# Other PSUM banks for one feed-forward block, another form of the RMS norm in two mixers, operand sums inside the first group of the kernel, and 24 matmuls ahead of it

## The chip, the cores and the metric

One core of a Trainium2 chip runs the whole program. The metric is device time in microseconds of one execution, from inputs in HBM to outputs in HBM. TensorE (PE) runs at one of two clocks, 1.2 or 2.4 GHz; the profile gives the granted one as a share of the upper.

## What is computed

A trunk of two macaron layers over x of shape (1, 512, 1024) in float32, each layer a half-weighted SwiGLU feed-forward block, a mixer, and another half-weighted feed-forward block:

```
def rmsnorm(x, g):
    y = x * lax.rsqrt(jnp.mean(x * x, axis=-1, keepdims=True) + EPS)
    return y * g

def swiglu(x, w_in, w_out):            # w_in (1024, 2*2816), w_out (2816, 1024)
    gate, up = jnp.split(x @ w_in, 2, axis=-1)
    return (jax.nn.silu(gate) * up) @ w_out

for i in range(2):                      # mixer 0: attention over keys that an indexer picks; mixer 1: gMLP
    h = h + 0.5 * swiglu(rmsnorm(h, norm_g[i, 0]), ffn_w_in[i, 0], ffn_w_out[i, 0])
    h = h + mixer_i(rmsnorm(h, norm_g[i, 1]))
    h = h + 0.5 * swiglu(rmsnorm(h, norm_g[i, 2]), ffn_w_in[i, 1], ffn_w_out[i, 1])
return rmsnorm(h, final_g)
```

## The kernel before

**Layout.** Activations lie transposed: eight tiles `H[j]`, each 128 features by 512 tokens. Every product is made of three float32r matmuls (`mul3`, L366 to L368): operand x and weight w are split into a high part (`xh`, `whi`, a rounding copy on ScalarE, ACT) and the rest (`xl`, `wlo`, a subtraction on VectorE, DVE), and PE adds wh·xh, wh·xl and wl·xh into one PSUM bank. `prepare(j)` (L321) makes `xh`, `xl` and the squares of one tile; the opening of the kernel does it by `weigh` and `square` (L302, L308). `H` itself is not scaled by the norm before a product: the token's 1/rms is multiplied onto the product afterwards (`R["b"]`).

**Weights.** `WeightStream` brings weights in units of eight 128x128 pieces in the exact order of use. SP's queue loads a unit into one of four `raw` tiles, ACT makes `whi` (L183), DVE `wlo` (L186). For plain units the converted parts have three places: a unit is converted only when PE has left the unit three before it. The program is written out by hand; each engine executes its instructions strictly in the order in which the code issues them.

**A feed-forward block** (`ffn`, L409), four of them, for layer and norm numbers 0, 2, 3 and 5: a first `group` takes four products at once, eight k-steps of twelve matmuls; then four `single` products; then nine `two_pairs`, each seven products (f0 to f6) of 24 matmuls of 256 columns, a Strassen-like form that uses sums of halves of the operands (`TH`, `TL`, made by `sums`, L441, four sets, one for each pair of tiles); and three times an output product into `H` (`add`, L640: DVE reads the bank at L642, adds at L643, then `finish` prepares that tile for the next stage). Blocks two to four make three sets at k-steps 5 to 7 of their first group and the fourth behind the first `single`; the first block makes one set behind each of its four singles.

**PSUM** is two sets of four banks, tags `acc` and `aux`, each handed out in turn. A block begins with four `acc` banks for its first group and takes `aux` for the singles. Its last product ends on `acc` for features 4 to 7, and the group of what follows begins on `acc` too, both between the second and third feed-forward block and between the third block and the gMLP mixer.

**Norms.** In the feed-forward blocks the sum of squares over features is made by columns (`scale_columns`, L391: four float32 matmuls of one column, which show as eight instructions), the reciprocal root on a 128x4 tile (L292 to L297), and the spread over all partitions by `scale_rows` (L399). The mixers use `token_scale` (L341): two float32r matmuls with a matrix of ones that sum all 512 columns into every partition, the root on a 128x512 tile, and later `as_columns` (L354), four transposes, for the factor by token.

**The opening.** SP's queue loads the first weight unit in two halves, the tiles `H[j]` and three more units; the norm gains `g_sb` come by the queue of GpSimd (POOL).

Of the kernel before, what the change touches and what calls it, by code (L numbers as in the profile page):

```python
# [50 lines left out]
LAST = 2 * CHUNKS[-1]  # L51
N_LOADS = sum(4 if k == "S" else 1 for k in PLAN)
# [188 lines left out]
def tile_trunk(ctx: ExitStack, tc, specs_out, xT, wst, gT, gl, rel, onehot, bu, bv, lng, lnb, wspT, bsp, out):  # L241
# [29 lines left out]
    pad(small, 32)  # L271
    g_sb = const.tile([P, 7, KD], F32, name="g_sb")
    nc.gpsimd.dma_start(g_sb, gT)
# [11 lines left out]
    nc.scalar.activation(ones_r, ones, AF.Copy)  # L285

# [54 lines left out]
    def token_scale(tag="aux"):  # L341

        ah = small.tile([P, S], F32R, tag="s0_512", bufs=1, name=uname("ah"))
        al = small.tile([P, S], F32R, tag="s1_512", bufs=1, name=uname("al"))
        nc.scalar.activation(ah, acc[0], AF.Copy)
        nc.vector.tensor_tensor(al, acc[0], ah.bitcast(F32), op=ALU.subtract)
        ps = bank(tag)
        mm(ps, ones_r, ah, start=True, stop=False)
        mm(ps, ones_r, al, start=False, stop=True)
        v = small.tile([P, S], F32, tag="ms", bufs=1, name=uname("ms"))  # L350
        nc.vector.tensor_scalar(v, ps, 1.0 / D, EPS, op0=ALU.mult, op1=ALU.add)
        return rsqrt(v, [P, S])

    def as_columns(rb):  # L354

        ps = bank("aux")
        for t in range(NT):
            nc.tensor.transpose(ps[:, t * P:(t + 1) * P], rb[:, t * P:(t + 1) * P], ident)
        c = small.tile([P, NT], F32, tag="rcol", bufs=1, name=uname("rcol"))
        nc.vector.tensor_copy(c, ps.rearrange("p (t q) -> p t q", q=P)[:, :, 0])  # L360
        return c

# [28 lines left out]
    def scale_columns(ps):  # L391

        for t in range(NT):
            mm(ps[:, t:t + 1], acc[0][:, t * P:(t + 1) * P], ones[:, :1], start=True, stop=True)
        v = small.tile([P, NT], F32, tag="vcol", bufs=1, name=uname("vcol"))
        nc.vector.tensor_scalar(v, ps[:, :NT], 1.0 / D, EPS, op0=ALU.mult, op1=ALU.add)
        return rsqrt(v, [P, NT])

    def scale_rows(rc, ps):  # L399
# [4 lines left out]
        rh = small.tile([P, S], F32, tag="ms", bufs=1, name=uname("rh"))  # L404
        nc.scalar.activation(rb, ps, AF.Copy)
        nc.scalar.activation(rh, ps, AF.Copy, scale=0.5)  # L406
        return rb, rh

    def ffn(layer, which, norm, finish, begin=None, hooks=None, aside=None, last=None):  # L409
# [8 lines left out]
        KP = KD // 2  # L418
        n1, n2 = slice(0, HALF), slice(HALF, S)
        with tc.tile_pool(name=uname("ffn"), bufs=1) as fp:  # L420
# [67 lines left out]
            def plain_pairs(banks, g, begun=0):  # L488
                for i in range(begun, 2):
                    nc.vector.tensor_tensor(g[:, i], banks[2 * i], R["b"], op=ALU.mult)  # L490
# [66 lines left out]
            def scale():  # L557
                R["ps"] = R.get("ps") or bank("aux")
                R["c"] = scale_columns(R["ps"])
# [16 lines left out]
            rest = [bank("aux") for _ in range(2)]  # L576
            if not hooks:
                plain_pairs(banks, g[0])
            else:
                R["ps"] = bank("aux")  # L580
            single(rest[0], 2, KD, spec_in)
# [7 lines left out]
            rest.append(bank("aux"))  # L589
# [647 lines left out]
```

## Time and profile before

| | us |
|---|---|
| median of 3 runs (2110.95 to 2118.17) | 2111.97 |
| the profiled execution, its own time | 2112.86 |
| its span, first to last instruction | 2110.8 |
| PE busy | 2076.8 (98%) |
| DVE busy | 1487.5 (70%) |
| ACT busy | 891.3 (42%) |
| mean granted clock | 0.997 |

The stretches of the span on PE: opening group and singles 0 to 57 us, the rest of the first feed-forward block to 364, attention mixer to 626, second block to 974, third to 1326, gMLP mixer to 1749, fourth block to the end. Matmuls are pipelined: the next one starts before the modelled end of the one before, so a group's pace is read from starts.

### The profile page before, as it was taken

What the parts mean: (1) busy time and instruction counts of PE and PEld (TensorE: products, weight loads), DVE (VectorE), ACT (ScalarE), POOL (GpSimd) and SP (SyncE); (2) the same over time, 40 slices, a digit from 0 to 9 for tenths busy, and PEclk for the clock granted to TensorE, in tenths of its full rate; (3) what the DMA queues carried; (4) which work ended last, traced back from release to release, by engine and by line L of the source; (5) the groups of instructions that cost most, each with busy time, mean ns of one, the idle gap of its engine ahead of it and who ended that gap; (6) DMA issues with size and microseconds to landing.
All of it is one profiled execution on the core that took longest, in us unless ns stands there. A gap on an engine that the chain in (4) does not pass through costs nothing.

```text
span 2110.8 us, 29664 instructions
## 1 busy us (share of the span) xinstructions
PE 2076.8 (98%) x12208; PEld 1839.1 (87%) x12208; DVE 1487.5 (70%) x2044; ACT 891.3 (42%) x1151; POOL 78.8 (4%) x58
## 2 busy tenths in 40 slices
PE   8999999999999999999999999999999999999998
PEld 6889898788888999897889999788888888989897
DVE  6868686697767677676868677645746466768686
ACT  5535344434445345344625344322323245435253
POOL 0000000143200000000000000000000000000000
PEclk9999999999999999999999999999999999999999
DMA  4233332222122222222323222422232222323221
GB/s 172 97 116 109 110 110 99 90 96 94 61 80 100 100 100 101 100 100 80 108 95 117 100 101 80 141 100 80 91 109 80 91 90 90 108 93 110 104 96 70
DMA packets 58887, 209.70 MB, mean 99 GB/s; under 512 B 6696, under 2 KB 6760, under 8 KB 58624
## 3 DMA queue, kind: packets, MB, share of 16 engines
q1 hardware_dynamic: 55584, 198.73, 26.9%
q0 software_dynamic: 1440, 5.41, 0.8%
q10 hardware_dynamic: 1728, 3.67, 0.5%
q8 instruction: 95, 1.56, 0.3%
q14 instruction: 40, 0.33, 0.1%
HBM read 205.67 MB, written 4.74 MB: 100 GB/s over the span
## 4 chain that ended last, share of the span: by engine, by line
PE 88%; DVE 7%; ACT 3%; issue 2%; DMA 0%; ACTq 0%; DVEq 0%; POOLq 0%
PE acc L366 15%; PE acc L367 15%; PE acc L368 15%; PE aux L366 10%; PE aux L367 10%; PE aux L368 10%; DVE wlo L186 1%; ACT whi L183 1%; PE aux L979 1%; PE aux L980 1%; PE aux L981 1%; PE aux L1031 1%; PE acc L979 1%; PE acc L980 1%; PE acc L981 1%
## 5 line engine op out<-in xcount | busy, mean ns | idle before, releaser
L186 DVE TENSOR_TENSOR wlo<-raw,whi 128x1024 fp32r<-128x1024 f32 (+1 forms) x382 | 464.2, 1219 | 309.7 <-ACT whi L183 308.2
L183 ACT ACTIVATE whi<-raw 128x1024 fp32r<-128x1024 f32 (+1 forms) x409 | 426.5, 1050 | 485.1 <-PE acc L367 203.7
L366 PE MATMUL acc<-xh,whi 128*128 128x256 f32 (+1 forms) x888 | 305.7, 344 | 8.9 <-ACT xh L305 5.9
L367 PE MATMUL acc<-xl,whi 128*128 128x256 f32 (+1 forms) x888 | 296.4, 334 | 0.1
L368 PE MATMUL acc<-xh,wlo 128*128 128x256 f32 (+1 forms) x888 | 296.3, 334 | 0.0
L366 PEld LDWEIGHTS acc<-xh,whi 128*128 128x128 f32 x888 | 169.5, 191 | 27.5 <-ACT xh L305 5.9
L366 PE MATMUL aux<-xh,whi 128*128 128x256 f32 (+1 forms) x592 | 190.7, 322 | 1.2 <-ACT rh L406 1.2
L368 PE MATMUL aux<-xh,wlo 128*128 128x256 f32 (+1 forms) x592 | 190.5, 322 | 1.3 <-DVE wlo L186 1.3
L367 PE MATMUL aux<-xl,whi 128*128 128x256 f32 (+1 forms) x592 | 190.2, 321 | 0.0
L366 PE MATMUL acc<-th,whi 128*128 128x256 f32 x640 | 181.8, 284 | 7.5 <-ACT u L519 6.0
L367 PEld LDWEIGHTS acc<-xl,whi 128*128 128x128 f32 x888 | 169.5, 191 | 18.2 <-issue 1.4
L368 PEld LDWEIGHTS acc<-xh,wlo 128*128 128x128 f32 x888 | 169.3, 191 | 16.7
L367 PE MATMUL acc<-tl,whi 128*128 128x256 f32 x640 | 181.2, 283 | 0.4 <-DVE tl L389 0.4
L368 PE MATMUL acc<-th,wlo 128*128 128x256 f32 x640 | 181.1, 283 | 0.0
L366 PE MATMUL aux<-th,whi 128*128 128x256 f32 x512 | 144.9, 283 | 0.0
L367 PE MATMUL aux<-tl,whi 128*128 128x256 f32 x512 | 144.9, 283 | 0.0
L368 PE MATMUL aux<-th,wlo 128*128 128x256 f32 x512 | 144.9, 283 | 0.0
L366 PEld LDWEIGHTS acc<-th,whi 128*128 128x128 f32 x640 | 122.8, 192 | 8.5 <-ACT u L519 6.8
L366 PE MATMUL acc<-yh,whi 128*128 128x512 f32 x328 | 127.7, 389 | 0.0
L367 PE MATMUL acc<-yl,whi 128*128 128x512 f32 x328 | 127.7, 389 | 0.0
L366 PE MATMUL aux<-yh,whi 128*128 128x512 f32 x328 | 127.6, 389 | 0.0
L367 PE MATMUL aux<-yl,whi 128*128 128x512 f32 x328 | 127.6, 389 | 0.0
(296 smaller groups left out, 4383.1 us busy)
## 6 DMA issues: line engine op xcount, KB each, us to landing
raw<-in_wst SPq DMA_DIRECT2D x372, 512.0 KB, 3.3
dist<-dist_rows ACTq DMA_DIRECT2D x8, 320.0 KB, 4.3
h<-in_xT SPq DMA_DIRECT2D x8, 256.0 KB, 6.8
tb<-dist POOLq DMA_DIRECT2D x8, 256.0 KB, 3.8
bias<-in_bv POOLq DMA_DIRECT2D x1, 1536.0 KB, 7.5
raw<-in_wst SPq DMA_DIRECT2D x2, 256.0 KB, 3.3
wT<-in_wspT POOLq DMA_DIRECT2D x1, 512.0 KB, 9.3
bs<-in_bsp POOLq DMA_DIRECT2D x1, 512.0 KB, 11.3
```

Of the source, the lines that this page charges most:

```text
L183: self.nc.scalar.activation(hi[:, s], src[:, s], AF.Copy)
L186: self.lo_engine.tensor_tensor(lo[:, s], src[:, s], hi[:, s].bitcast(F32), op=ALU.subtract)
L366: mm(ps, wh, xh, start=first, stop=False, **kw)
L367: mm(ps, wh, xl, start=False, stop=False, **kw)
L368: mm(ps, wl, xh, start=False, stop=last, **kw)
L979: mm(banks[t], xh, wh, start=k == 0, stop=False)
L980: mm(banks[t], xl, wh, start=False, stop=False)
L981: mm(banks[t], xh, wl, start=False, stop=k == KD - 1)
L1031: mm(ps[:, t * P:(t + 1) * P], V[t][:, d * P:(d + 1) * P], wT[:, g, :], start=True, stop=True)
```

## The change

- The third feed-forward block is called with `tags=("aux", "acc")`: wherever a block takes `acc` it now takes `aux` and the other way round.
- `token_scale` and `as_columns` are gone. Both mixers use columns: three hooks of their first group split the squares (`parts_of_squares`), sum them by columns and spread them by rows at k-steps 4, 5 and 6. In feed-forward blocks the split stands at k-step 3.
- `scale_columns` takes the split squares: eight float32r matmuls with two columns of ones in place of four float32 ones with one column.
- The first block makes all four sets of operand sums inside its first group, at k-steps 4 to 7; its norm is summed after the first single and spread after the second, and the special copy of its first single's bank is gone.
- 24 matmuls of 128x128 ones stand ahead of all others on PE; `g_sb` is loaded by ACT's queue instead of POOL's; a pad in the pool `small` is 64 bytes instead of 32.

```
+WARM = 24
-    pad(small, 32)
+    pad(small, 64)
-    nc.gpsimd.dma_start(g_sb, gT)
+    nc.scalar.dma_start(g_sb, gT)
...
+    warm = bank("aux")
+    for _ in range(WARM):
+        mm(warm[:, :P], ones_r, ones_r, start=True, stop=True)
...
-    def scale_columns(ps):
+    def parts_of_squares():
+        ah = small.tile([P, S], F32R, tag="s0_512", bufs=1, name=uname("ah"))
+        al = small.tile([P, S], F32R, tag="s1_512", bufs=1, name=uname("al"))
+        split(acc[0], ah, al)
+        return ah, al
+
+    def scale_columns(ps, parts):
         for t in range(NT):
-            mm(ps[:, t:t + 1], acc[0][:, t * P:(t + 1) * P], ones[:, :1], start=True, stop=True)
+            for part in parts:
+                mm(ps[:, 2 * t:2 * t + 2], part[:, t * P:(t + 1) * P], ones_r[:, :2], start=part is parts[0],
+                   stop=part is parts[1])
...
+    def norm_hooks(R, ps, k):
+        def parts():
+            R["sq"] = parts_of_squares()
+        def columns():
+            R["c"] = scale_columns(ps, R["sq"])
+        def rows():
+            R["b"], _ = scale_rows(R["c"], ps, False)
+        return {k: parts, k + 1: columns, k + 2: rows}
...
             def hook(k):
                 if hooks:
                     hooks[k]()
-                elif k in (5, 7):
-                    (scale if k == 5 else spread)()
-                if k > 4 and not hooks:
-                    sums(k - 5)
+                elif k == 5:
+                    scale()
+                elif k == 7:
+                    spread()
+                elif k == 3:
+                    R["sq"] = parts_of_squares()
+                if k > 3 + (not hooks):
+                    sums(k - 4 - (not hooks))
-            banks = [bank() for _ in range(4)]
+            banks = [bank(tags[0]) for _ in range(4)]
...
             single(rest[0], 2, KD, spec_in)
-            sums(0) if hooks else sums(3)
+            if hooks:
+                R["sq"] = parts_of_squares()
+                scale()
+            else:
+                sums(3)
             step()
             single(rest[1], NJ + 2, KD, spec_in)
             if hooks:
-                scale()
-                sums(1)
+                spread()
+                plain_pairs(banks, g[0])
...
-            if hooks:
-                spread()
-                nc.vector.tensor_tensor(g[1][:, 0], rest[0], R["b"], op=ALU.mult)
-                plain_pairs(banks, g[0])
-                sums(2)
...
-            group([kw] + pq, ["kw"] + [QI0 + P * i for i in range(4)], KD, spec_a, hooks={4: scale})
+            group([kw] + pq, ["kw"] + [QI0 + P * i for i in range(4)], KD, spec_a, hooks=norm_hooks(R, ps, 4))
...
-    ffn(1, 0, 3, into(4))
+    ffn(1, 0, 3, into(4), tags=("aux", "acc"))
```

The order of instructions moves at three places that matter below. In the rows, numbers behind names tell buffers apart, and lines of the changed kernel are its own (its L348 to L350 are L366 to L368 before, L310 is L306, L187 is L186).

PE at the end of the second feed-forward block and the start of the third, before: the last matmuls of the output product, then the first group on four `acc` banks.

```order
L367 MATMUL acc_9007<-yl_8788,whi_8909 128x512
L368 MATMUL acc_9007<-yh_8787,wlo_8910 128x512
L366 MATMUL acc_9052<-xh_80,whi_8948 128x512
L367 MATMUL acc_9052<-xl_88,whi_8948 128x512
L368 MATMUL acc_9052<-xh_80,wlo_8949 128x512
L366 MATMUL acc_9053<-xh_80,whi_8948 128x512
```

The same place of PE after the change.

```order
L349 MATMUL acc_9053<-yl_8834,whi_8955 128x512
L350 MATMUL acc_9053<-yh_8833,wlo_8956 128x512
L348 MATMUL aux_9098<-xh_80,whi_8994 128x512
L349 MATMUL aux_9098<-xl_88,whi_8994 128x512
L350 MATMUL aux_9098<-xh_80,wlo_8995 128x512
L348 MATMUL aux_9099<-xh_80,whi_8994 128x512
```

The order of work is the same; the group no longer begins on the set of banks that the output product ends on.

DVE in the opening group, before: the operand rests `xl` of tiles 6 and 7, the adding of squares, and weight units 5 and 6 of the stream.

```order
L306 SCALAR_TENSOR_TENSOR xl_94<-h_77,g_sb,xh_86 128x512
L317 TENSOR_TENSOR sqacc_171<-sqacc_171,sq_304 128x512
L186 TENSOR_TENSOR wlo_308<-raw_183,whi_307 128x1024
L306 SCALAR_TENSOR_TENSOR xl_95<-h_78,g_sb,xh_87 128x512
L317 TENSOR_TENSOR sqacc_171<-sqacc_171,sq_329 128x512
L317 TENSOR_TENSOR sqacc_171<-sqacc_171,sq_344 128x512
L186 TENSOR_TENSOR wlo_353<-raw_208,whi_352 128x1024
```

DVE at the same place after the change, from the last row of the first set of sums on.

```order
L371 TENSOR_TENSOR tl_168<-u_32_318,th_164 128x512
L310 SCALAR_TENSOR_TENSOR xl_94<-h_77,g_sb,xh_86 128x512
L321 TENSOR_TENSOR sqacc_196<-sqacc_196,sq_343 128x512
L455 TENSOR_TENSOR u_36_348<-m_34_346 128x256
L456 TENSOR_TENSOR u_36_348<-m_35_347,m_34_346 128x256
L457 TENSOR_TENSOR u_37_349<-m_35_347,u_36_348 128x256
L458 TENSOR_TENSOR u_37_349<-m_35_347,u_37_349 128x256
L371 TENSOR_TENSOR tl_169<-u_36_348,th_165 128x512
L371 TENSOR_TENSOR tl_169<-u_37_349,th_165 128x512
L187 TENSOR_TENSOR wlo_361<-raw_208,whi_360 128x1024
L310 SCALAR_TENSOR_TENSOR xl_95<-h_78,g_sb,xh_87 128x512
```

One set of sums, six instructions, now stands ahead of `xl` of tile 6, and a second one ahead of `xl` of tile 7. On ACT the high parts `xh` of the same tiles stand behind the same sets.

PE in the attention mixer's first group, before: the end of k-step 4, the two matmuls of `token_scale`, the start of k-step 5.

```order
L368 MATMUL aux_3497<-xh_84,wlo_3529 128x512
L348 MATMUL acc_3601<-ah_3597,ones_r 128x512
L349 MATMUL acc_3601<-al_3598,ones_r 128x512
L366 MATMUL acc_3493<-xh_85,whi_3528 128x512
L367 MATMUL acc_3493<-xl_93,whi_3528 128x512
```

PE there after the change: the end of k-step 5, the column sums, the start of k-step 6. Behind k-step 6 four instructions of `scale_rows` follow.

```order
L350 MATMUL aux_3531<-xh_85,wlo_3563 128x512
L384 MATMUL acc_3527<-ones_r,ah_3631 128x2
L384 MATMUL acc_3527<-ones_r,al_3632 128x2
L384 MATMUL acc_3527<-ones_r,ah_3631 128x2
L384 MATMUL acc_3527<-ones_r,al_3632 128x2
L384 MATMUL acc_3527<-ones_r,ah_3631 128x2
L384 MATMUL acc_3527<-ones_r,al_3632 128x2
L384 MATMUL acc_3527<-ones_r,ah_3631 128x2
L384 MATMUL acc_3527<-ones_r,al_3632 128x2
L348 MATMUL acc_3526<-xh_86,whi_3562 128x512
```

The sums stand one k-step, fifteen matmuls, behind the split of the squares instead of right behind it.

## Rows read from the trace of the kernel before

**Rows 1.** Part 1 of the page: busy time, share of the span, instructions.
```profile
PE 2076.8 (98%) x12208; PEld 1839.1 (87%) x12208; DVE 1487.5 (70%) x2044; ACT 891.3 (42%) x1151; POOL 78.8 (4%) x58
```

**Rows 2.** Timeline of PE, third block's start: start, duration, instruction [idle before, releaser].
```profile
975.16 0.39 PE L367 MATMUL acc<-xl,whi 128*128 128x512 f32 x1
975.39 0.39 PE L368 MATMUL acc<-xh,wlo 128*128 128x512 f32 x1
977.19 0.50 PE L366 MATMUL acc<-xh,whi 128*128 128x512 f32 x1 [1.42 <-DVE gate L642]
...
979.79 0.50 PE L366 MATMUL acc<-xh,whi 128*128 128x512 f32 x1 [1.63 <-DVE gate L642]
```

**Rows 3.** Timeline of PE, the start of the gMLP mixer.
```profile
1329.45 0.50 PE L979 MATMUL acc<-whi,xh 128*128 128x512 f32 x1 [1.42 <-DVE gate L642]
...
1332.04 0.50 PE L979 MATMUL acc<-whi,xh 128*128 128x512 f32 x1 [1.63 <-DVE gate L642]
```

**Rows 4.** Windows: stretch, length, busy us (instructions) by engine, granted clock, DMA.
```profile
383.68:387.10 3.42, 3.42 (x10) 2.65 (x9) 3.25 (x6) 0.00 (x0) 0.00 (x0) 0.50 0.35 135
...
977.50:981.00 3.50, 1.87 (x8) 1.23 (x7) 3.46 (x6) 1.75 (x3) 0.00 (x0) 1.00 0.45 150
...
1332.60:1336.00 3.40, 3.40 (x9) 2.63 (x8) 3.40 (x6) 2.19 (x3) 2.65 (x5) 0.50 0.45 112
```

**Rows 5.** Timeline of DVE at the third block's start, tile 7 and a weight unit.
```profile
981.64 0.74 DVE L333 SCALAR_TENSOR_TENSOR xl<-h,g_sb,xh 128x512 fp32r<-128x512 f32 x1
...
982.91 1.22 DVE L186 TENSOR_TENSOR wlo<-raw,whi 128x1024 fp32r<-128x1024 f32 x1
```

**Rows 6.** Timeline of PE, norms of the attention mixer and, last, the gMLP mixer.
```profile
380.53 0.39 PE L368 MATMUL aux<-xh,wlo 128*128 128x512 f32 x1
...
383.02 0.50 PE L349 MATMUL acc<-al,ones_r 128*128 128x512 f32 x1 [0.84 <-DVE al L346]
383.36 0.39 PE L366 MATMUL acc<-xh,whi 128*128 128x512 f32 x1
...
401.32 0.60 PE L358 MATMUL aux<-ident,nwy 128*128 128x128 f32 x4
...
1346.15 0.50 PE L349 MATMUL aux<-al,ones_r 128*128 128x512 f32 x1 [0.40 <-DVE al L346]
```

**Rows 7.** Timeline of PE, norm by columns in the third feed-forward block.
```profile
994.21 0.95 PE L394 MATMUL aux<-ones,sqacc 128*128 128x1 f32 x8
...
1000.56 1.05 PE L402 MATMUL aux<-ident,nwy 128*128 128x128 f32 x8
```

**Rows 8.** The opening: issue of the fourth weight unit, and `xl` of tile 3.
```profile
5.93 0.71 SPq L107 DMA_DIRECT2D raw<-in_wst  x1
...
16.75 0.75 DVE L306 SCALAR_TENSOR_TENSOR xl<-h,g_sb,xh 128x512 fp32r<-128x512 f32 x1
```

**Rows 9.** View by tile (raw), window of that one issue: time to landing.
```profile
DMA to landing us min/median/max: 8.5/8.5/8.5
```

**Rows 10.** Windows in the opening, columns as in rows 4.
```profile
6.00:9.00 3.00, 3.00 (x7) 2.02 (x8) 2.07 (x3) 1.76 (x3) 0.00 (x0) 1.00 0.98 330
```

**Rows 11.** Timeline of DVE and ACT: `xl` of tile 7, and one set of sums.
```profile
28.75 0.75 DVE L306 SCALAR_TENSOR_TENSOR xl<-h,g_sb,xh 128x512 fp32r<-128x512 f32 x1
...
54.03 1.32 ACT L446 ACTIVATE m<-h,g_sb 128x512 f32<-128x512 f32 x2
...
56.52 1.48 DVE L389 TENSOR_TENSOR tl<-u,th 128x512 fp32r<-128x512 f32 x2
```

**Rows 12.** Timeline of PE: f0 and f4 of the first pairs, first and second block.
```profile
57.22 0.28 PE L366 MATMUL acc<-xh,whi 128*128 128x256 f32 x1
...
73.99 0.39 PE L366 MATMUL acc<-th,whi 128*128 128x256 f32 x1 [2.72 <-ACT u L519]
...
671.73 0.28 PE L366 MATMUL acc<-xh,whi 128*128 128x256 f32 x1
...
684.49 0.39 PE L366 MATMUL acc<-th,whi 128*128 128x256 f32 x1 [1.08 <-ACT u L519]
```

More of the change, by code (lines that the diff above doesn't have):

```diff
@@ L339, in prepare @@
             behind_it.pop(0)()
[L341 to L361, printed above, removed]
     def mul3(ps, w, x, first, last, **kw):
@@ L403, in scale_rows, with ffn @@
         rb = small.tile([P, S], F32, tag="nwy512", bufs=1, name=uname("rb"))
-        rh = small.tile([P, S], F32, tag="ms", bufs=1, name=uname("rh"))
+        rh = small.tile([P, S], F32, tag="ms", bufs=1, name=uname("rh")) if halves else None
         nc.scalar.activation(rb, ps, AF.Copy)
-        nc.scalar.activation(rh, ps, AF.Copy, scale=0.5)
+        if halves:
+            nc.scalar.activation(rh, ps, AF.Copy, scale=0.5)
         return rb, rh
-    def ffn(layer, which, norm, finish, begin=None, hooks=None, aside=None, last=None):
+    def norm_hooks(R, ps, k):
[6 more added lines that the diff above has]
+        return {k: parts, k + 1: columns, k + 2: rows}
+    def ffn(layer, which, norm, finish, begin=None, hooks=None, aside=None, last=None, tags=("acc", "aux")):
         NJ = DFF // P
         KP = KD // 2
+        tag_of = lambda i: tags[i % 2]
         n1, n2 = slice(0, HALF), slice(HALF, S)
@@ L486, in flush, with plain_pairs @@
                     later.pop(0)()
-            def plain_pairs(banks, g, begun=0):
-                for i in range(begun, 2):
+            def plain_pairs(banks, g):
+                for i in range(2):
                     nc.vector.tensor_tensor(g[:, i], banks[2 * i], R["b"], op=ALU.mult)
@@ L557, in scale @@
             def scale():
-                R["ps"] = R.get("ps") or bank("aux")
-                R["c"] = scale_columns(R["ps"])
+                R["ps"] = R.get("ps") or bank(tags[1])
+                R["c"] = scale_columns(R["ps"], R["sq"])
             def spread():
@@ L585, in ffn @@
             if hooks:
[L586 to L587 removed]
+                spread()
+                plain_pairs(banks, g[0])
             step()
[L589 removed]
+            rest.append(bank(tags[1]))
             single(rest[2], 3, KD, spec_in)
[L591 to L595 removed]
             step()
[L597 removed]
+            rest.append(bank(tags[1]))
             single(rest[3], NJ + 3, KD, spec_in)
[L599 to L600 removed]
             flush()
@@ L613, in ffn @@
                     if n_dp == 0:
-                        between = [lambda: plain_pairs(rest, g[1], 1 if hooks else 0)]
+                        between = [lambda: plain_pairs(rest, g[1])]
                     if aside:
@@ L618, in ffn @@
                         between = last[0](bank("acc"), gate_tile)
-                    two_pairs(pair, "aux" if n_dp % 2 else "acc", between)
+                    two_pairs(pair, tag_of(n_dp), between)
                     n_dp += 1
@@ L622, in ffn @@
                 n_k = done - p0
-                tag0 = "aux" if n_dp % 2 else "acc"
-                tag1 = "acc" if n_dp % 2 else "aux"
+                tag0 = tag_of(n_dp)
+                tag1 = tag_of(n_dp + 1)
                 def spec_out(k, c, p0=p0):
@@ L773, in mixer_a @@
                         continue
[L774 removed]
+                    rc = R["c"]
                     nc.vector.tensor_scalar(rq, rc, P ** -0.5, None, op0=ALU.mult)
@@ L971, in mixer_b @@
                                         pattern=[[0, GROUPS], [1, P]], channel_multiplier=-1)
+                hooks = norm_hooks(R, bank("aux"), 4)
                 for c in range(6):
```

25 lines of the change are left out of this document (9 added, 16 removed).

## The prediction

> **What bounds the kernel now.** I read the page's busy times first: PE works 98% of the span and no other engine over 70% [rows 1]. So the time is PE's work plus about 34 us in which it stands, plus what a low clock adds; an edit counts only by what it takes from or adds to PE's own stream. Then the waits of PE and its timeline around each. They are few and local: the opening, the starts of the third block and of the gMLP mixer [rows 2, 3], the attention mixer's norm [rows 6], and a stall in the first pair of forms of every block [rows 12]. Last the granted clock by windows, because two of these places are followed by a stretch at the lower of the two levels [rows 4].
>
> **Swapped banks, third block.** In [rows 2] PE starts a matmul every 0.23 us (975.16 to 975.39), then waits until DVE has read an output bank: the third and fourth banks of the new group are those of features 6 and 7. The idles are 1.42 and 1.63 us. Each counts from the modelled end, 0.39 after a start, where the next start was due after 0.23, so each lost 0.16 more: 3.4 us. With the swap the group takes banks that were read ten microseconds earlier. What is late next? PE would need tile 7 at k-step 7, twelve matmuls of 0.23 times seven after 974.25, at 993.3; it is ready at 982.4. The third weight unit is needed at k-step 4, at 985.1, and its `wlo` ends at 984.1 [rows 5]; DVE's backlog there does not depend on PE, so this stays. Slack 1.0 us, no new wait. Taken: **-3.4**; bounds -3.4 and, if that slack fails, -2.4.
>
> **The same at the gMLP mixer.** The third block now ends on `aux`, and the mixer begins on `acc`: the same two idles, 1.42 and 1.63 [rows 3], **-3.4**. Behind them the clock stands at 0.50 for 3.4 us, with PE busy all the time [rows 4]; half of that is lost: **-1.7**. The clock fell after idles that go away, so I take it as gone; at the third block the same idles left it at 1.00 [rows 4], so it is a matter of where they fall, and a fall elsewhere is possible.
>
> **Norm of the attention mixer.** Before: from 380.53 + 0.23 = 380.76, where the next product was due, to 383.36: 2.6 us, most of it waiting for the split of the squares that stands right ahead of it [rows 6]; then 3.4 us at clock 0.50, 1.7 lost [rows 4]; and four transposes, 0.60. Together 4.9. After: columns and rows as the feed-forward blocks have them, 0.95 and 1.05 [rows 7]. The split now has a k-step of fifteen matmuls, 3.4 us, before its use, and the small root (a dozen instructions on 128x4 tiles in place of eleven on 128x512) another; PE waits for neither. **-2.9**. The root leaves DVE some 5 us; DVE isn't late there, so that earns nothing.
>
> **Norm of the gMLP mixer.** Before: 0.40 of waiting, two matmuls and their 0.16 [rows 6], 1.1, and the transposes 0.6; after 2.0: **+0.3**.
>
> **Column sums in float32r.** Eight instructions of two columns are nowhere in the trace. The float32 ones of one column, also eight on the page, take 0.95 together [rows 7], nearly all weight loading, as a load of 128x128 stands before each: the upper bound. Four transposing passes in 0.60 [rows 6] are the lower one. I take 0.95, the row with the same load and next to the same columns: 0 for each of the four feed-forward blocks. The lower bound would give 0.35 at six places, -2.1. The split adds 0.6 us each on ACT and DVE at k-step 3, beside eight microseconds in which neither has other work there: 0.
>
> **Warm-ups and the gains' queue.** The first twelve real matmuls run at one start in 0.43 us (seven in 3.0 us [rows 10]; the clock column isn't filled that early). At full clock and with the gains some 0.4 us earlier, PE would be through k-step 2 about 2.8 us earlier. But k-step 3 needs `xl` of tile 3, which ends at 17.50 [rows 8]. ACT makes its `xh` behind the fourth weight unit, whose load is issued at 5.93 and lands 8.5 us later, at 14.4 [rows 8, 9], with the DMA engines full (0.98) [rows 10]; nothing of that is PE's. PE just waits longer there: **0**. At best the whole 2.4 of the slow dozen come through; at worst PE, idle for nearly 3 us between 14.3 and 17.5, loses the clock again, +1.7.
>
> On this the Trainium skill (TensorE: Matmul & The Clock Gate, Part 1) says that the engine starts throttled and that sustained activity releases it. The trace agrees with the clock's behaviour; by that rule alone the opening would gain 2.4 us. The same page (HAM oscillation) warns that idle stretches between bursts throttle it again, and that speaks against holes such as this one.
>
> **Sums inside the first group.** One set takes 4.0 us from ACT's first scaling (54.03) to DVE's last difference (56.52 + 1.48) [rows 11], ACT and DVE by turns; ACT is free for the next thing 3.2 us after the start. Now one set stands ahead of tile 6 and a second one and a weight unit ahead of tile 7. Counted through: the first set starts behind `sq` of tile 4 at 22.3, waits for DVE until 24.0 and lets `xh` of tile 6 go at 26.1; `xl` is ready at 27.6, where PE wants it at 26.7. The second set runs 27.3 to 31.2, the weight unit's copy at 30.4, `xh` of tile 7 31.4 to 32.1, `xl` (behind that unit's `wlo`) to 33.4. Before it was ready at 29.5 [rows 11]: 3.9 later, and PE ends the group at 33.4 + 11 x 0.23 = 35.9. Sets three and four run beside k-step 7 and the first single (24 x 0.23 = 5.5, to 41.4) and end at 40.5; then a weight unit and the split of the squares, 42.7, for which the column sums wait 1.3 us. 43.5 after the sums, 49.0 after the second single, 49.9 after the rows, and two singles later, at 60.8, f0 starts: 57.2 before [rows 12], **+3.6**. What comes back: from f0 to f4 the first block takes 73.99 - 57.22 = 16.8 us, because f2 waits for sums and f4 for copies behind them on ACT and DVE; the second block, whose sums are done by then, takes 684.49 - 671.73 = 12.8. That is **-4.0**. Opening together **-0.4**; the bounds are the chain's overlaps, -2 to +2.
>
> **Sum.** -3.4 - 3.4 - 1.7 - 2.9 + 0.3 + 0 + 0 - 0.4 = -11.5, a half per cent. Against the profiled execution's own 2112.86 that gives 2101.4; that run stands 0.9 above the median 2111.97, against which it gives **2100.5**. The pad moves small tiles and costs nothing that a row shows.
>
> **Rivals.**
> - *The opening loses the clock.* PE stands nearly 3 us ahead of 17.5 and 3.1 us ahead of 33.4. A fall at the first costs 1.7 and delays the chain behind it; one at the second is half hidden by the wait for the squares. 2102.2 to 2104. For it: [rows 4], where shorter idles sufficed twice; against: the same idles at 977 did not.
> - *The banks were not the limit*: with them free, PE waits for DVE's backlog (tile 7 or the third weight unit) for most of the 6.8 us. 2107. Against: the slack in [rows 5].
> - *Warm-ups pay*: tile 3 is ready earlier than its DMA chain says, 2.4 more: 2098.1. The chain of [rows 8, 9] speaks against it.
> - *Columns are cheap*: two-column sums at the lower bound, 2098.4.
> - *The sums put the opening in series* (the slower side): ACT and DVE hand over so badly that all four sets, 4 x 4.0, stand ahead of tile 7 or of the norm: f0 starts 16 us later instead of 3.6, with two falls of the clock, +15.8: 2116.3. It decides from the point where PE stands over 15 us in the opening; the orders of ACT and DVE show only two sets ahead of tile 7.
>
> **How the numbers follow.** Forecast 0.50, the clock in the opening 0.20, cheap columns 0.10, warm-ups 0.08, banks not the limit 0.08, sums in series 0.04. A measurement of this kernel tells about 0.5% from no change; the line is 2101.4. Three quarters of the forecast lie below it, with cheap columns and warm-ups: faster 0.56. The rest of the forecast and the other rivals are within 0.5%: 0.42. Slower by more: 0.02. The range reaches over the bounds of columns and opening and over a lost clock: 2096.5 to 2105.
>
> **What would show it.** Right: no wait for L642's banks at the starts of the third block and the gMLP mixer, no granted clock under 1 there or near 384; in the opening, `xl` of tile 3 at 17.5 as before in spite of a full clock, tile 7 near 33.4, f0 near 61, f4 within 13 us of f0. Wrong: tile 7 ready at 30 or at 37, a wait of PE for `wlo` at the third block's k-step 4, column sums far from 0.95, or a stretch at half clock in the opening.

## The result, and the profile after

| | before | after |
|---|---|---|
| median, us | 2111.97 (2110.95 to 2118.17) | 2101.51 (2101.08 to 2101.77) |
| profiled execution, us | 2112.86 | 2101.77 |
| its span, us | 2110.8 | 2099.8 |

The ratio is 0.9945 (95% interval 0.9931 to 0.9960), 10.5 us less; 2100.5 was forecast. The kernel before takes 2110.4 to 2114.4 in executions with a mean granted clock of 0.997 or 0.998 and 2115.8 to 2118.5 in those with 0.994 or 0.995; the changed kernel's five all show 0.999 and lie within 0.7 us. PE now fills 99% of its span, against [rows 1].

```profile
PE 2078.5 (99%) x12252; PEld 1844.2 (88%) x12252; DVE 1477.4 (70%) x2046; ACT 894.0 (43%) x1157; POOL 78.1 (4%) x57
```

To see where the time went, I took the same matmul in both traces at the borders of the stages, and compared how long each stage took.

| stage on PE | ends at, before | after | change | predicted |
|---|---|---|---|---|
| opening, to f4 of the first pair | 73.99 | 74.60 | +0.6 | -0.4 |
| from there to the attention mixer | 363.75 | 364.36 | 0 | 0 |
| attention mixer and second block | 974.25 | 972.26 | -2.6 | -2.9 |
| third block | 1326.51 | 1320.85 | -3.7 | -3.4 |
| start and norm of the gMLP mixer | 1355.31 | 1344.50 | -5.1 | -4.8 |
| the rest, to the end of the span | 2110.8 | 2099.8 | -0.2 | 0 |

The start of the third block, timeline of PE after the change: the first group's first, second, third and fourth bank, each with its first matmul; then the third and fourth bank at the start of the gMLP mixer. The idles of [rows 2] and [rows 3] are gone; a matmul starts every 0.23 us.

```profile
972.26 0.39 PE L348 MATMUL aux<-xh,whi 128*128 128x512 f32 x1
972.94 0.39 PE L348 MATMUL aux<-xh,whi 128*128 128x512 f32 x1
973.62 0.39 PE L348 MATMUL aux<-xh,whi 128*128 128x512 f32 x1
974.30 0.39 PE L348 MATMUL aux<-xh,whi 128*128 128x512 f32 x1
...
1322.21 0.39 PE L984 MATMUL acc<-whi,xh 128*128 128x512 f32 x1
...
1322.89 0.39 PE L984 MATMUL acc<-whi,xh 128*128 128x512 f32 x1
```

The windows of after that answer to [rows 4], with the same columns (the granted clock is the third figure from the right): attention norm, third block, gMLP mixer. All stand at 1.00.

```profile
383.00:387.00 4.00, 4.00 (x23) 3.47 (x22) 1.62 (x8) 0.00 (x0) 0.00 (x0) 1.00 0.36 131
972.00:977.00 5.00, 5.00 (x23) 4.13 (x22) 3.97 (x6) 2.38 (x4) 0.00 (x0) 1.00 0.34 119
1326.00:1331.00 5.00, 5.00 (x23) 4.14 (x23) 4.96 (x8) 3.15 (x4) 3.19 (x6) 1.00 0.44 125
```

The column sums of the third block (timeline of PE, the first three of eight) start 0.03 and then 0.11 us apart. All eight take 0.81 us from the first to the next product, where the float32 ones of [rows 7] took 0.81: no difference, as predicted.

```profile
988.58 0.17 PE L384 MATMUL acc<-ones_r,ah 128*128 128x2 f32 x1
988.61 0.25 PE L384 MATMUL acc<-ones_r,al 128*128 128x2 f32 x1
988.72 0.25 PE L384 MATMUL acc<-ones_r,ah 128*128 128x2 f32 x1
```

The opening is the one stage that went the other way. Timelines of after: PE (the warm-ups and the first real matmul), ACT (the conversion of the fourth weight unit), DVE (`xl` of tiles 3 and 7), PE again (f0 and f4).

```profile
2.90 5.38 PE L289 MATMUL aux<-ones_r 128*128 128x128 f32 x24 [2.90 <-ACT ones_r L286]
8.09 0.73 PE L348 MATMUL acc<-xh,whi 128*128 128x512 f32 x1
...
16.05 1.06 ACT L184 ACTIVATE whi<-raw 128x1024 fp32r<-128x1024 f32 x1 [3.56 <-PE acc L349]
...
18.29 0.74 DVE L310 SCALAR_TENSOR_TENSOR xl<-h,g_sb,xh 128x512 fp32r<-128x512 f32 x1
...
34.10 0.75 DVE L310 SCALAR_TENSOR_TENSOR xl<-h,g_sb,xh 128x512 fp32r<-128x512 f32 x1
...
62.29 0.28 PE L348 MATMUL acc<-xh,whi 128*128 128x256 f32 x1
...
74.60 0.39 PE L348 MATMUL acc<-th,whi 128*128 128x256 f32 x1 [0.64 <-ACT u L526]
```

The warm-ups last until the first real matmul at 8.09; before the change that one began at 5.89. PE leaves the first weight unit late, so ACT cannot reuse its place for the fourth until 16.05, and `xl` of tile 3, made behind that, ends at 19.03 instead of 17.50 [rows 8].

### The profile page after: what moved, and what is told of

Same layout as the page of the kernel before. It is cut to its first block, busy times and chain, and to the rows that moved or that the text cites. A ratio compares the mean times of both kernels' runs of the same rounds, so it can differ in the third digit from the quotient of the medians.

```text
span 2099.8 us, 29764 instructions
## 1 busy us (share of the span) xinstructions
PE 2078.5 (99%) x12252; PEld 1844.2 (88%) x12252; DVE 1477.4 (70%) x2046; ACT 894.0 (43%) x1157; POOL 78.1 (4%) x57
## 4 chain that ended last, share of the span: by engine, by line
PE 90%; DVE 5%; ACT 3%; issue 1%; ACTq 0%; DVEq 0%
PE acc L348 15%; PE acc L350 15%; PE acc L349 15%; PE aux L348 11%; PE aux L349 11%; PE aux L350 11%; PE acc L984 1%; PE aux L986 1%; PE aux L984 1%; PE acc L986 1%; PE acc L985 1%; PE aux L985 1%; PE aux L1034 1%; ACT whi L184 1%; PE acc L902 1%
## 5 line engine op out<-in xcount | busy, mean ns | idle before, releaser
L187 DVE TENSOR_TENSOR wlo<-raw,whi 128x1024 fp32r<-128x1024 f32 (+1 forms) x382 | 463.4, 1218 | 301.9 <-ACT whi L184 300.7
L348 PE MATMUL acc<-xh,whi 128*128 128x512 f32 (+1 forms) x864 | 299.0, 346 | 1.7 <-ACT xh L309 1.6
L349 PE MATMUL acc<-xl,whi 128*128 128x512 f32 (+1 forms) x864 | 289.4, 335 | 1.1 <-DVE xl L310 1.1
L350 PE MATMUL acc<-xh,wlo 128*128 128x512 f32 (+1 forms) x864 | 289.4, 335 | 0.4 <-DVE wlo L187 0.4
L350 PE MATMUL aux<-xh,wlo 128*128 128x256 f32 (+1 forms) x616 | 196.7, 319 | 0.8 <-DVE wlo L187 0.8
L348 PE MATMUL aux<-xh,whi 128*128 128x256 f32 (+1 forms) x616 | 196.9, 320 | 0.0
L348 PEld LDWEIGHTS acc<-xh,whi 128*128 128x128 f32 x864 | 165.0, 191 | 20.0 <-ACT xh L309 2.6
L350 PEld LDWEIGHTS acc<-xh,wlo 128*128 128x128 f32 x864 | 164.7, 191 | 17.6 <-DVE wlo L187 0.8
L348 PE MATMUL acc<-th,whi 128*128 128x256 f32 x608 | 172.6, 284 | 2.8 <-ACT u L526 2.8
L350 PE MATMUL acc<-th,wlo 128*128 128x256 f32 x608 | 172.0, 283 | 0.0
L349 PE MATMUL acc<-tl,whi 128*128 128x256 f32 x608 | 172.0, 283 | 0.0
L348 PE MATMUL aux<-th,whi 128*128 128x256 f32 x544 | 154.0, 283 | 1.1 <-ACT u L526 1.1
L349 PE MATMUL aux<-tl,whi 128*128 128x256 f32 x544 | 153.9, 283 | 0.0
L350 PE MATMUL aux<-th,wlo 128*128 128x256 f32 x544 | 153.9, 283 | 0.0
L348 PE MATMUL acc<-yh,whi 128*128 128x512 f32 x328 | 127.7, 389 | 0.0
L348 PE MATMUL aux<-yh,whi 128*128 128x512 f32 x328 | 127.6, 389 | 0.0
L350 PE MATMUL acc<-yh,wlo 128*128 128x512 f32 x328 | 127.6, 389 | 0.0
```

What stands on the lines that cost most here:

```text
L187: self.lo_engine.tensor_tensor(lo[:, s], src[:, s], hi[:, s].bitcast(F32), op=ALU.subtract)
L348: mm(ps, wh, xh, start=first, stop=False, **kw)
L349: mm(ps, wh, xl, start=False, stop=False, **kw)
L350: mm(ps, wl, xh, start=False, stop=last, **kw)
```

## Experiments

Times are medians; the changed kernel's is 2101.51. The kernels ran in several batches, in which the kernel before had medians of 2111.97 to 2113.01, so a difference of less than a microsecond between batches rests on the traces and not on the medians.

**The warm-ups.** The prediction said that they change nothing. The trace of after says that they cost. The first kernel leaves them out.

```
-    warm = bank("aux")
-    for _ in range(WARM):
-        mm(warm[:, :P], ones_r, ones_r, start=True, stop=True)
```

> The changed kernel without its 24 warm-up matmuls. Its trace has the first real matmul at 8.09 us (5.89 before the change), the clock at 1.00 from 13.34 (11.63 before) and xl of tile 3 at 19.04 (17.50 before), because ACT's conversion of the fourth weight unit waits for PE there. Theory now: the warm-ups only delay PE, so without them the first matmul starts near 5.9, the clock rises near 11.6, xl of tile 3 ends near 17.5, and f0 starts 1.0 to 1.5 earlier than 62.29; time 2100.0 to 2100.5. The prediction's own term (warm-ups cost and give nothing): 2101.5, f0 at 62.3, because DVE's chain of operand sums sets the pace behind k-step 3. A rival for the clock: without warm-ups it rises later than 13.3, and the time is above 2101.5.

2100.61 (2099.69 to 2101.45). Timelines of PE, DVE and PE:

```profile
5.81 0.80 PE L344 MATMUL acc<-xh,whi 128*128 128x512 f32 x1 [5.81 <-ACT xh L305]
...
16.32 0.74 DVE L306 SCALAR_TENSOR_TENSOR xl<-h,g_sb,xh 128x512 fp32r<-128x512 f32 x1
...
60.33 0.28 PE L344 MATMUL acc<-xh,whi 128*128 128x256 f32 x1
```

Tile 3 is ready at 17.06, and everything behind it keeps its distance: f0 starts 43.3 us later in both kernels. So the narrow warm-ups cost 2.0 us in this pair of traces. The profiled execution of the changed kernel is the latest of its kind: in the six profiled executions that begin with the same warm-ups, `xl` of tile 3 ends between 17.89 and 19.03, and in the three without them and with the same order on ACT between 16.96 and 17.09, so the cost lies between 0.8 and 2.1. By the medians it is 0.9, with overlap: two of the four executions without warm-ups took 2099.7 and 2099.9, the other two 2101.3 and 2101.5, at a lower mean granted clock (0.997 against 0.999).

The second kernel asks whether any warm-up can work, with wide matmuls.

```
-WARM = 24
+WARM = 7
+    wide_r = XL[KD - 1]
+    nc.vector.tensor_scalar(wide_r.rearrange("p (a b) -> p a b", b=P),
+                            ones.unsqueeze(1).broadcast_to([P, NT, P]), 1.0, None, op0=ALU.mult)
...
-        mm(warm[:, :P], ones_r, ones_r, start=True, stop=True)
+        mm(warm, ones_r, wide_r, start=True, stop=True)
```

> The changed kernel with 7 warm-up matmuls of 512 columns in place of 24 of 128 columns. They should take 7 x 0.43 = 3.0 us, from 2.9 to about 5.9, so that the first real matmul starts at 5.9 as before the change. If such matmuls do for the clock what the real ones did (5.74 us after the first real one before the change, 5.25 after in the changed kernel), it rises at about 8.4, PE is through k-step 2 about 1.5 us earlier and stands there until xl of tile 3 ends at 17.5, as the prediction argued for any warm-up: the time is that of the kernel without warm-ups, 2100.0 to 2100.5. Rival one, a warm-up that works pays: xl of tile 3 earlier than 17.0 and a time under 2099.5. Rival two: the clock rises no earlier than 11 us, nothing is gained by any warm-up, 2100.0 to 2101.5. Rival three: the hole ahead of tile 3 brings the clock down again, a stretch at 0.50 behind 17 us and 1.7 more.

2100.07 (2099.89 to 2101.46), no different from no warm-ups (2100.61). Timelines of PE, then ACT, then PE at k-steps 3 and 7, and the window behind:

```profile
2.91 3.36 PE L291 MATMUL aux<-xl,ones_r 128*128 128x512 f32 x7 [2.91 <-ACT ones_r L286]
6.06 0.72 PE L350 MATMUL acc<-xh,whi 128*128 128x512 f32 x1
...
14.09 1.06 ACT L184 ACTIVATE whi<-raw 128x1024 fp32r<-128x1024 f32 x1 [1.56 <-DMA raw<-in_wst]
...
17.13 0.50 PE L351 MATMUL acc<-xl,whi 128*128 128x512 f32 x1 [0.80 <-DVE xl L312]
...
32.94 0.75 PE L351 MATMUL acc<-xl,whi 128*128 128x512 f32 x1 [0.81 <-DVE xl L312]
...
33.01:36.42 3.41, 3.41 (x8) 2.69 (x9) 3.28 (x8) 2.38 (x5) 0.00 (x0) 0.50 0.87 308
```

The starts of PE go from 0.43 to 0.23 us apart at 9.1. PE comes early to k-step 3 and waits: ACT now stands for the DMA of the fourth unit, which the prediction named as the limit, and tile 3 is ready at 17.07 as without warm-ups. The hole ahead of tile 7 is followed by a fall of the clock here, as the prediction's rival had it for the opening.

**The swapped banks**, undone.

```
-    ffn(1, 0, 3, into(4), tags=("aux", "acc"))
+    ffn(1, 0, 3, into(4))
```

> The changed kernel with the third feed-forward block on its old sets of banks. Theory: the idles of 1.42 and 1.63 us for L642's banks (other line number here) come back at the starts of the third block and of the gMLP mixer, 3.65 us at each by the two traces (3.4 was predicted), and with those at the mixer the 3.4 us at half clock, 1.7: +9.0, 2110.5. Rival: the clock fell there for another reason than these idles (the mixer's own norm, which is different now), and stays at 1.00: +7.3, 2108.8. Second rival: the third block's idle brings a fall as well, since its start now stands at another time: +10.7, 2112.2.

2109.88 (2109.17 to 2110.29): +8.4. The waits are back (timeline of PE), but the fall of the clock is behind the first pair of them, at the third block, and not at the gMLP mixer as before the change (windows, at either place):

```profile
974.57 0.50 PE L348 MATMUL acc<-xh,whi 128*128 128x512 f32 x1 [1.42 <-DVE gate L649]
...
977.16 0.50 PE L348 MATMUL acc<-xh,whi 128*128 128x512 f32 x1 [1.61 <-DVE gate L649]
...
1331.00 0.50 PE L984 MATMUL acc<-whi,xh 128*128 128x512 f32 x1 [1.63 <-DVE gate L649]
...
977.90:981.31 3.41, 3.41 (x9) 2.65 (x9) 3.41 (x5) 2.17 (x3) 0.00 (x0) 0.50 0.00 0
...
1331.50:1335.00 3.50, 3.50 (x17) 2.86 (x17) 3.50 (x6) 2.70 (x4) 2.69 (x6) 1.00 0.43 109
```

By the traces 5.2 at the third block and 3.6 at the mixer, less 0.7 because this execution's clock rose earlier in the opening. None of the expectations had it so: in this profiled execution, as in that of the kernel before, the idles bring one fall, at one of the two places.

**The sums**, put behind the singles again, with the early norm left in.

```
-                if k > 3 + (not hooks):
-                    sums(k - 4 - (not hooks))
+                if k > 4 and not hooks:
+                    sums(k - 5)
...
                 scale()
+                sums(0)
...
                 plain_pairs(banks, g[0])
+                sums(1)
...
             single(rest[2], 3, KD, spec_in)
+            if hooks:
+                sums(2)
...
             single(rest[3], NJ + 3, KD, spec_in)
+            if hooks:
+                sums(3)
```

> The changed kernel with the first block's four sets of operand sums behind its four singles again, one each, as before the change (the early norm stays; warm-ups stay). It tells the price of the sums inside the first group apart from that of the warm-ups. The prediction had -0.4 for the sums: so here +0.4, 2101.9, with f0 some 3.5 us earlier (near 58.8) and f4 4 us later after f0. The two traces give the opening +0.6 together; if the warm-ups take 1.4 of that, the sums gave -0.8, and this kernel takes 2102.3. Rival: the sums cost more than they give back and the warm-ups cost nothing, this kernel takes 2100.9 or less.

2104.76 (2104.26 to 2105.17): +3.2, more than expected (+2.4 by the traces). Timeline of PE: f0, the wait for the second sums in f2, and f4:

```profile
56.26 0.28 PE L348 MATMUL acc<-xh,whi 128*128 128x256 f32 x1
...
65.45 0.43 PE L348 MATMUL acc<-th,whi 128*128 128x256 f32 x1 [4.04 <-ACT th L370]
...
76.85 0.39 PE L348 MATMUL acc<-th,whi 128*128 128x256 f32 x1 [1.72 <-ACT u L526]
```

f0 starts 6 us earlier, but f4 follows after 20.6 us instead of 12.3, with a fall of the clock behind the 4.04. It isn't the old order (there the norm came after two singles, and the same stretch took 16.8): with the early norm the first gates stand ahead of the second set of sums on DVE, with the old one they stood ahead of the third. So the early norm and the sums inside the group belong together; the old norm with the sums inside was not tried.

**Better places for the sums.** With the warm-ups out, two orders between these extremes. The first has two sets in the group, behind the operands of tile 7, and two behind singles.

```
-                if k > 3 + (not hooks):
-                    sums(k - 4 - (not hooks))
+                if k > 4 + bool(hooks):
+                    sums(k - 5 - bool(hooks))
...
                 scale()
+                sums(2)
...
                 plain_pairs(banks, g[0])
+                sums(3)
```

> The changed kernel without warm-ups, with the first two sets of operand sums at k-steps 6 and 7, behind the operands of the last tile, and the other two behind the first and second single. Theory: tile 7 is ready near 28.5 instead of 32.9, the group ends 3.5 to 4 us earlier, f0 starts near 57; from f0 to f4 some 14 to 16 us in place of 12.3 because the last two sets and their copies are late for f2 and f4. So the end of the first pair moves by -2 to 0: 2098.5 to 2100.6. Rival: each set behind a single costs more than it saves, as when all four stood there (20.6 us from f0 to f4): 2101 to 2102.

2099.64 (2098.92 to 2100.02): f0 at 56.53, but f4 14.7 us later, with this wait and a fall of the clock behind it:

```profile
71.24 0.38 PE L344 MATMUL acc<-th,whi 128*128 128x256 f32 x1 [3.04 <-ACT u L522]
```

The second has them as the other three blocks do.

```
-                if k > 3 + (not hooks):
-                    sums(k - 4 - (not hooks))
+                if k > 4:
+                    sums(k - 5)
...
                 scale()
+                sums(3)
```

> The changed kernel without warm-ups, with sets of operand sums at k-steps 5, 6 and 7 and the fourth behind the first single, as the other feed-forward blocks have them: one set ahead of the operands of tile 7 in place of two, none ahead of tile 6. Theory: tile 7 ready near 29.8 instead of 32.9, the group ends 2 to 3 us earlier, the norm as before that, f0 near 58.5, and f0 to f4 within 12.3 to 13.3: -1.5 to -2.5 against the kernel without warm-ups, 2098 to 2099. Rival: ACT and DVE are full until f4 whatever the order, f4 starts at 72.6 as without this edit, and the time is the same, 2100.0 to 2100.6.

2097.03 (2096.60 to 2097.32), better than expected. Timelines of DVE (`xl` of tile 7) and PE (f0):

```profile
29.44 0.74 DVE L306 SCALAR_TENSOR_TENSOR xl<-h,g_sb,xh 128x512 fp32r<-128x512 f32 x1
...
57.63 0.28 PE L344 MATMUL acc<-xh,whi 128*128 128x256 f32 x1
```

`xl` of tile 7 ends at 30.18 (32.88 without this edit), and f4 starts 12.3 us behind f0. The second set ahead of tile 7 cost the 2.6 us that come back here between `xl` of tile 3 and f0 (40.7 us in place of 43.3), and nothing is lost behind it.

**The norms of the mixers**, put back in both.

```
...
-            group([kw] + pq, ["kw"] + [QI0 + P * i for i in range(4)], KD, spec_a, hooks=norm_hooks(R, ps, 4))
+            group([kw] + pq, ["kw"] + [QI0 + P * i for i in range(4)], KD, spec_a, hooks={4: scale})
...
-                    rc = R["c"]
+                    rc = R["c"] = as_columns(rb)
...
-                        if c == 0 and k in hooks:
-                            hooks[k]()
+                        if c == 0 and k == 4:
+                            R["b"] = token_scale()
+                        if c == 0 and k == KD - 1:
+                            R["c"] = as_columns(R["b"])
```

> The changed kernel with the norm of both mixers made by token_scale and as_columns again (sums over all 512 columns into every partition, four transposes for the factor by token); all else as changed. The prediction's terms: +2.9 in the attention mixer (1.2 of waits and transposes and 1.7 of a stretch at half clock behind them) and -0.3 in the gMLP mixer, so 2104.1 against 2101.5. Rival: the clock fall of the attention mixer does not come back, since in other runs it moved between places, and the time is 2102.4. The two traces so far give 2.6 for the attention mixer and nothing for the other.

2115.27 (2114.81 to 2115.90): +13.8, which neither expectation had. The old norm itself accounts for under 3 us of it; every output product of every feed-forward block is slower. The old norm brings a small tile back, while the wider pad stays, so the tiles behind it in the blocks' and mixers' own pools lie 32 bytes further on. Two kernels tell this apart: the changed kernel with the old pad, and the old norm under the old pad.

```
-    pad(small, 64)
+    pad(small, 32)
```

> The changed kernel with the pad in the pool of small tiles at 32 bytes, as before the change; nothing else differs, no instruction is added or moved. The prediction put the pad at nothing: 2101.5. The run with the mixers' old norm under the new pad took 2115.3, and in its trace the matmuls of 512 columns on yh and yl stand 0.233 us apart in place of 0.227 (1968 of them, 12.7 us), those of 256 columns on tl and th 0.117 to 0.119 in place of 0.120 (2304, -4.7 us). New theory: that was the pad, since the tile that the old norm brings back moves all behind it by 32 bytes, and the same shows here, from the other side: a pace of 0.233 for yh and a time of 2110 to 2116. Rival: the old norm itself did it (by what it issues), and the time here is 2101.5.

2110.94 (2110.58 to 2111.20): +9.4, by 32 bytes of padding, with the same instructions in the same order. Where the old norm stands under this pad, in the same batch, matmuls on `yh` are 0.227 apart again. The first output product of the first block, 96 matmuls from one start to the other, on PE of the changed kernel (21.79 us, 0.2270 each):

```profile
103.49 0.40 PE L348 MATMUL acc<-yh,whi 128*128 128x512 f32 x1
...
125.28 0.39 PE L348 MATMUL aux<-yh,whi 128*128 128x512 f32 x1
```

and of this one (22.40 us, 0.2333 each):

```profile
102.82 0.39 PE L348 MATMUL acc<-yh,whi 128*128 128x512 f32 x1
...
125.22 0.40 PE L348 MATMUL aux<-yh,whi 128*128 128x512 f32 x1
```

> The changed kernel with the norm of both mixers made by token_scale and as_columns again, now under the pad of 32 bytes that stood beside that norm before the change, so that all tiles behind it lie where they lay. If the 13.8 us of the first try were the place of the tiles, this kernel takes 2104.1 (the prediction's terms, +2.9 and -0.3, with a fall of the clock in the attention mixer) or 2102.4 (without the fall), and matmuls on yh stand 0.227 apart. Rival: the norm itself costs them, 2115.

2104.48 (2103.67 to 2105.86): +3.0, near the 2.6 at which the prediction priced the two norms (+2.1 by the traces). With the 9.4 of the pad that makes 12.4 of the 13.8; what the rest is stays open. And the reason is another than the prediction's. There is no fall at the attention norm here (window), and still the mixer takes 2.5 us longer, because PE waits later on for DVE (timelines of PE and DVE; the last row is the end of the small root after the change):

```profile
383.00:387.00 4.00, 4.00 (x18) 3.32 (x19) 3.31 (x6) 0.00 (x0) 0.00 (x0) 1.00 0.35 131
...
382.98 0.50 PE L353 MATMUL acc<-al,ones_r 128*128 128x512 f32 x1 [0.85 <-DVE al L350]
...
407.43 0.50 PE L844 MATMUL aux<-wlo,xh 128*128 128x512 f32 x1 [1.09 <-DVE wi L813]
...
390.97 0.69 DVE L301 SCALAR_TENSOR_TENSOR nwy<-nwt,nwy 128x512 f32<-128x512 f32 x1
...
405.75 1.66 DVE L813 TENSOR_SCALAR wi<-wi 128x32 f32<-128x32 f32 x1
...
387.93 0.16 DVE L301 SCALAR_TENSOR_TENSOR nwy<-nwt,nwy 128x4 f32<-128x4 f32 x1
```

The root on 128x512 keeps DVE until 391.7, after the change the small one until 388.1, and the chain on DVE from there to `wi` at L813 sets when PE may go on. Before the change the half clock at the norm had made PE so late that it did not wait there.

**The opening again.** What held up the wide warm-ups was an order on ACT: `xh` of tile 3 stands behind the conversion of a unit that k-step 6 uses first. On top of the better place of the sums I moved tile 3 ahead of it, without warm-ups and with seven wide ones.

```
-        if k + 1 < KD:
-            weigh(k + 1, 0)
+        for j in {1: (2, 3), 2: ()}.get(k, (k + 1,)):
+            if j < KD:
+                weigh(j, 0)
```

> The kernel with sums at k-steps 5 to 7 and without warm-ups (2097.0), with one more edit: xh and xl of tile 3 are made ahead of the conversion of the third and fourth weight unit, behind tile 2. The fourth unit isn't used before k-step 6, but ACT made xh of tile 3 behind it, and xl ended at 17.0. Theory: xl of tile 3 ends near 12.5, so k-step 3 is no longer bound by it; without warm-ups PE comes there at 15.7 to 16.8 anyway, so 0 to -0.3: 2096.7 to 2097.1. Rival: the third unit or tile 4 are late by it, +0.5 to +1.

2096.16 (2095.74 to 2096.58), 0.9 less where 0.3 at most was expected. `xl` of tile 3 ends at 12.5, k-step 3 has no wait, and `xl` of tile 7 comes a microsecond earlier, at 29.10, which the expectation had left out.

> The same with 7 warm-up matmuls of 512 columns ahead of all others. The warm-ups alone brought the clock up at 9.1 us (13.3 in the changed kernel) and PE to k-step 3 at 14.35, where it stood for tile 3 until 17.07: a gain of nothing, as the prediction argued. If that tile was what hid it, the gain comes now: k-step 3 without a wait, PE 1.5 to 2.4 us ahead at k-step 4; but tile 7, ready at 30.2 by DVE's chain, then holds PE longer, so 0.5 to 1.5 less, 2095.5 to 2096.5. Rival one: DVE's and ACT's chain up to tile 7 takes all of it, 2097.0. Rival two: the hole ahead of tile 7 brings the clock down, 2098 or more.

2095.61 (2095.32 to 2095.79). PE is ahead, but `xl` of tile 7 is ready at 28.93 against 29.10, and PE waits for it:

```profile
28.99 0.51 PE L350 MATMUL acc<-xl,whi 128*128 128x512 f32 x1 [0.81 <-DVE xl L311]
```

So warm-ups that work are worth 0.5 us by the medians, with ranges that touch, and 0.1 by the traces (f0 at 56.52 and 56.38): DVE's chain takes the rest, at tile 7 now instead of tile 3.

**The place of the sums' tiles.** The last kernel takes up the 32 bytes: `TH` and `TL` are moved by them, on top of the sums at k-steps 5 to 7, the early tile 3 and the wide warm-ups. The tiles `yh` and `yl` behind them move by 64 bytes with this edit; all other operands of matmuls stay.

```
-            pad(fp, 352 if begin else 448)
+            pad(fp, 384 if begin else 480)
...
             TL = [fp.tile([P, 4, HALF], F32R, name=uname("tl")) for _ in range(KP)]
+            pad(fp, 32)
...
-            pad(fp, 256)
+            pad(fp, 192)
```

> The kernel with the sums at k-steps 5 to 7, tile 3 early and wide warm-ups (2095.6), with the tiles TH and TL of the operand sums moved by 32 bytes in each feed-forward block and no other matmul operand moved against the 64-byte grid. With the pad of 32 bytes, all operands in the blocks' own pools lay 32 bytes off from the weights of the ring that plain units use. There the 512-column matmuls whose activations and weights lie so took 233.3 ns from start to start in place of 226.8 (yh and yl, 1967 of them), but the 256-column ones with the two lying differently took 117.1 (xh, xl) and 118.5 ns (th, tl) in place of 120. Theory: it is the place of the one operand against the other that counts, and for 256 columns different places are the faster ones. Then the 3456 matmuls of 256 columns on th and tl gain 1.7 to 2.9 ns each, 5.9 to 10.0 us, and no other form changes: 2085.6 to 2089.7. Rival: what counts is the place of the weights alone (the faster ones above with weights off the old place), and th and tl at 120 as before: 2095.6. Second rival: DVE and ACT are slowed by the new place when they write the sums, 2096 to 2097.

2093.16 (2092.73 to 2093.28): the fastest of all, 19.1 less than the kernel before in the same batch (ratio 0.9905, 0.9888 to 0.9921), but a gain of 2.5 and not 6 to 10. From start to start matmuls of `tl` with `whi` take 116.0 ns and of `th` with `wlo` 118.3 (120 before), of `th` with `whi` nearly as long as before: some 7 us less together. But those of `yh` with `wlo` take 231.7 and of `yl` with `whi` 229.1 instead of 227: all on y together give some 4 us back. The same output product takes 21.99 us:

```profile
97.46 0.40 PE L349 MATMUL acc<-yh,whi 128*128 128x512 f32 x1
...
119.45 0.39 PE L349 MATMUL aux<-yh,whi 128*128 128x512 f32 x1
```

So my rule of two places 32 bytes apart is too simple. What in the addresses sets the pace stays open; `TH` and `TL` moved with the y tiles left in place was not tried.

## Why the prediction came out as it did

- **Swapped banks: right.** 3.7 at the third block and, with the clock, 5.1 at the gMLP mixer. What the profile calls idle is short of what is lost: a wait of 1.42 also slows the first matmul behind it (0.50 in place of 0.39), 0.1 each.
- **The clock behind the idles: right in the sum, half right in the mechanism.** The idles bring a fall, the swap takes it away. But it isn't tied to the mixer: with the swap undone it came at the third block, a shift that the prediction had called possible.
- **Norm of the attention mixer: right sum (2.6 for 2.9), wrong step.** The prediction counted 1.7 for the clock and nothing for DVE, because "DVE isn't late there". It is: without the fall PE waits 1.09 for `wi` at 407. The small root is what earns those microseconds.
- **Norm of the gMLP mixer and column sums: right within a few tenths.** The norm took 0.1 more by the traces of before and after and some 0.2 less by that with the old norm, where +0.3 was predicted; the column sums 0.
- **Sums inside the first group: right to a few tenths.** Counted from the end of `xl` of tile 3, f0 was predicted 43.3 us later and came 43.3 later; tile 7 15.9 and came 15.8. f0 to f4 took 12.3 (12.8 predicted). As a term that is -0.9 instead of -0.4.
- **Warm-ups: wrong step.** The prediction took for granted that they bring the full clock before the real matmuls, and asked only what that would be worth. They did not: 24 of them were followed by a dozen more at 0.43 us, and the clock rose 10.4 us after the first of them. They lasted longer than the stretch that PE had free, so they pushed back the first matmul, by it the place of the fourth weight unit, and by that tile 3: +1.5 against the kernel before in this profile (+0.4 to +1.3 in the other five that begin so), in place of 0. Its bounds (-2.4 to +1.7) held it by luck: the +1.7 was the price of a fall of the clock there, which did not come.
- **The pad: right for a reason that was not seen.** It "costs nothing" because it keeps every tile behind it where it was, when the old norm's small tile goes. Left out, it would have cost 9.4 and turned the whole gain into 1 us.

The parts sum to -11.0 in the span, where -11.5 was forecast, and the lost half microsecond is the warm-ups' 1.5 less what the banks, the sums and the rest gave beyond their terms. That it is no more is luck: errors of both signs met. Of the rivals, the fall of the clock in the opening is not in the profile of the changed kernel, but it stood in those of two close relatives (the wide warm-ups, the old norm under the old pad), behind the hole ahead of tile 7. PE did not stand ahead of tile 3 for the nearly 3 us that the prediction counted on: in the changed kernel the warm-ups made it late too, and with the wide ones it waited 0.80.

## What to carry to other kernels

Work that is put ahead of the first real instruction has to fit into time in which its engine waits anyway, and has to be shown to do what it is for: here the pace of the first real matmuls said at once that it did not. When a step is taken out, look which engine comes next at the following meeting point, since a wait that was hidden behind a slow clock takes its place. And a kernel whose tiles change in number or size has moved all the tiles behind them: hold their addresses still while you compare two versions, or you measure the addresses.

## What the hardware showed that was not expected

- **The place of operands sets the pace of matmuls.** 32 bytes of padding made some 2700 matmuls of 512 columns slower (from 226.8 to 233.3 ns for those on y) and some 6000 of 256 columns 1.3 ns shorter on average: about +17 and -8 us. By the addresses that the build gives out, all operands of these matmuls lie in the changed kernel at 32 past a multiple of 64 bytes; under the old pad those in the pools of the blocks and mixers lie at 0, and the x tiles and the weights of plain units still at 32.
- **The clock does not rise at a fixed time.** In six profiled executions that begin with the same 24 narrow warm-ups, the starts of real matmuls went from 0.43 to 0.23 us apart between 2.9 and 5.3 us after the first of them (10.95 to 13.34 in the span); in five without warm-ups, between 4.0 and 5.7 us. With the same warm-ups, that alone moves `xl` of tile 3 by 1.1 us from one execution to the next.
- **The clock falls behind some holes only.** Holes of 1.4 and 1.6 us, one behind the other, brought a stretch of 3.4 us at half clock at one of two like places, and at the other one in another kernel. The hole ahead of tile 7, of about the same length, brought one in two kernels and none in five.
